# Gates and branch projections of a hybrid mixer: from weights on the partitions to tokens on the partitions

## The chip, the cores and the metric

The kernel runs on one core of one Trainium2 chip. The time is device time in microseconds of one execution, as the median of several runs of the same program. The engines are named as in the profile: PE is the matmul engine (PEld its weight loads), DVE the vector engine, ACT the scalar engine, POOL the general engine, and SP the engine whose queue issues the DMA transfers here. A matmul has a stationary operand of 128 x 128 (loaded by PEld) and a moving one with up to 512 columns that streams past it.

## The reference, cut to what matters

The model is a trunk of two layers on 256 tokens of width 1024. Each layer is a feed-forward network (FFN), a mixer block with three branches, and a second FFN. Of the mixer block this part is concerned:

```python
(z, xbc, dt_raw, rq, rk, rv, rg, aq, ak, av, gate) = jnp.split(h @ w_in[l], offsets, axis=-1)
y_ssd = ssd_mixer(...); y_ret = retention_mixer(...); y_att = swa_sink_attention(...)
ys = jnp.stack([y_ssd, y_ret, y_att], axis=2)
branch = jnp.einsum('blmc,mcd->blmd', ys, w_branch[l])
gates = jax.nn.sigmoid((gate + b_gate[l]).reshape(bsz, L, N_BRANCH, D_MODEL))
y = jnp.sum(gates * branch, axis=2) @ w_out[l]
x = x + rmsnorm(y, mix_post_g[l])
```

Here `h` is the normed input (256 x 1024), each of the three gates and of the three branch projections is a product of 256 x 1024 by 1024 x 1024, and the gated sum goes through one more such product, `w_out`.

## The kernel before

Everything is float32. A product is made of three matmuls on split operands: `split` (lines 65 to 68) makes a high part by a rounding copy on ACT and the rest by a subtraction on DVE, and `mm3` (85 to 89) adds low x high, high x high and high x low. So each k slot of 128 rows costs three matmuls, at lines 87, 88 and 89.

Weights are streamed once. `units` (70 to 83) loads 512 KB into a buffer `raw` (four of them) and splits it into a buffer `hl` (eight of them); one `hl` holds two k slots of 512 columns. The activations lie transposed in four tiles (`xT` for the normed input, `yT` for a branch's output, `ysT` for the gated sum), high and low part, with features on the partitions and all 256 tokens in the columns; `transposed` (138 to 149) makes such tiles on PE from a tile with tokens on the partitions, four transposes to a PSUM bank, and splits them on ACT and DVE.

There are two forms of a product. `gemm` (91 to 98) has 128 tokens as the stationary operand and 512 weight columns as the moving one; the result has tokens on the partitions. `gemmT` (100 to 105) has 128 weight columns as the stationary operand and all 256 tokens as the moving one; the result has features on the partitions.

In `mix`, the projections of the mixers come first. Their tasks run as generators that `pump` moves on a step after each product. Then a loop over the mixers (m = 2 attention, 1 retention, 0 SSD) makes the gate (two halves of 512 columns), finishes the mixer, transposes its output to `yT`, and makes the branch projection. Gates and branches are `gemmT` products: the gate's bias is then one number to a partition and goes into ACT's tanh (line 763), the gated sum `acc` has features on the partitions, and it needs only a split to be the operand `ysT` of the output projection. `close` (276 to 284) makes the output projection in four `gemm` products (half, token tile), and norms each token tile behind its second half; the next phase's opening norm and transposes (`prenorm`, 154 to 163) follow on it.

PSUM has five banks for products (`acc`) and three for the rest (`pst`). The rows of weights that are broadcast to all partitions, 512 KB each (`gain`, 115 to 118), share two buffers. The order of instructions on each engine is not the program's own: the tile framework sorts them by a simulated timeline when the program is built, and each engine then works in order. All loads go through SP's queue, in order.

Of the kernel before, what the change touches and what calls it, by code (L numbers as in the profile page):

```python
# [8 lines left out]
F32 = mybir.dt.float32  # L9
R = mybir.dt.float32r  # L10
AF = mybir.ActivationFunctionType
ALU = mybir.AluOpType
AX = mybir.AxisListType

P = 128
T = 256
NT = 2
# [22 lines left out]
class Trunk:  # L40
# [11 lines left out]
        self.pst = pool("pst", 3, space=bass.MemoryType.PSUM)  # L52
        self.gens = []

# [1 line left out]
    def t4(self, shape, dtype=F32, name="t4"):  # L56
        return self.big.tile([P] + shape, dtype, tag="t4", name=name, bufs=N4)

# [39 lines left out]
        return ps  # L98

    def gemmT(self, ps, xT, slots, c0):  # L100
        """the transposed product: 128 columns of the weight from c0 on, by all tokens"""
        for k, (wh, wl) in enumerate(slots):
            x = xT[k // 2]
            cs = slice(c0, c0 + P)
            self.mm3(ps, wh[:, cs], wl[:, cs], x[:, k % 2, 0], x[:, k % 2, 1], k == 0, k == len(slots) - 1)
# [97 lines left out]
    def pbank(self, dtype=F32):  # L203
        return self.pst.tile([P, 4, P], dtype, tag="pst", name="pb")

# [1 line left out]
    def setup(self):  # L207
        nc, A = self.nc, self.A
        self.ready = False
# [55 lines left out]
        return t  # L265

    def begin(self, gname, l):
        """norm and transposes that open a phase: returns the tiles and what does one token tile"""
        g = self.gain(gname, l)
        xT = self.new_T(4, "xT")  # L270
        return xT, lambda t: self.prenorm(xT, t, g)
# [2 lines left out]
        return sum((self.units(self.A[f"w_ffn{i}_out"][l], u, fine=u > 8) for u in range(11)), [])  # L274

    def close(self, order, gemm, gpost, scale, nxt):
        """output projection, residual update and the next phase's opening, token tile by token tile"""
        y = {}
        for n, t in order:
            y[t, n] = gemm(n, t)  # L280
            if n:
                self.postnorm(t, [y[t, 0], y[t, 1]], gpost, scale, 4 * EPS, nxt is None)
                if nxt:
                    nxt(t)
# [34 lines left out]
        self.nc.sync.dma_start(out=b, in_=src)  # L319
        return b  # L320

# [1 line left out]
    def att_kv(self, t, ps):  # L323
        nc, S = self.nc, self.S
        if t == 0:
# [95 lines left out]
        for t in range(NT):  # L421
            S[f"y2{t}"] = o[t].rearrange("p h d -> p (h d)")

# [1 line left out]
    def rotate(self, key, t, ps):  # L425
        nc, S = self.nc, self.S
        ps = ps.rearrange("p (h o d) -> p h o d", h=4, o=2)
# [81 lines left out]
            S[f"y1{t}"] = y  # L509

    def silu2(self, ps, dtype=F32, name="gz"):
        """2 * silu of a PSUM bank, in a new SBUF tile"""
        nc = self.nc
        g = self.t2([512], name=name)
        nc.scalar.activation(out=g, in_=ps, func=AF.Tanh, scale=0.5)
        nc.vector.scalar_tensor_tensor(out=g, in0=g, scalar=1.0, in1=ps, op0=ALU.add, op1=ALU.mult)
        return g

# [1 line left out]
    def ssd_dt(self):  # L520
        nc, S = self.nc, self.S
        x = S["dt"]
# [143 lines left out]
    def mixer_consts(self, l):  # L666
        nc, A = self.nc, self.A
        c = lambda n, w: self.sm.tile([P] + w, F32, tag="mc_" + n, bufs=1, name=n)
        bc = lambda ap: ap.partition_broadcast(P)
        self.sink, self.ea, self.dsk, self.dtb = (c(n, [16]) for n in ("sink", "ea", "dsk", "dtb"))  # L670
        for t, n in ((self.sink, "attn_sinks"), (self.ea, "a_log"), (self.dsk, "d_skip"), (self.dtb, "dt_bias")):
            nc.sync.dma_start(out=t, in_=bc(A[n][l]))
        nc.scalar.activation(out=self.ea, in_=self.ea, func=AF.Exp)
        self.bg = c("bg", [24])
        nc.sync.dma_start(out=self.bg, in_=A["b_gate"][l])
        nc.vector.tensor_scalar(out=self.bg, in0=self.bg, scalar1=0.5, scalar2=None, op0=ALU.mult)
        self.cw = c("cw", [12, 5])
        nc.sync.dma_start(out=self.cw, in_=A["w_conv"][l])
        nc.vector.tensor_scalar(out=self.cw, in0=self.cw, scalar1=0.5, scalar2=None, op0=ALU.mult)

    def mix(self, l, xT, nxt):
# [57 lines left out]
        for key in ("rg0", "rg1"):  # L739
            slots = W(ci)  # L740
            ci += 1
            for t in range(NT):
                main(key, t, slots)
        acc = [self.t4([4, T], name="ysum") for n in range(2)]
        ysT = []
        for m, gens in ((2, att), (1, ret), (0, ssd)):
            if m == 1:
                for key in ("z0", "z1"):
                    slots = W(ci)
                    ci += 1  # L750
                    for t in range(NT):
                        main(key, t, slots)
            gate = []
            for n in range(2):
                slots = W(ci)
                ci += 1
                for b in range(2):
                    ps = self.acc.tile([P, 2, T], F32, tag="acc", name="acc")
                    g = self.t2([2, T], name="gate")
                    for j in range(2):  # L760
                        c = 4 * n + 2 * b + j
                        self.gemmT(ps[:, j], xT, slots, (2 * b + j) * P)
                        nc.scalar.activation(out=g[:, j], in_=ps[:, j], func=AF.Tanh, scale=0.5,  # L763
                                             bias=self.bg[:, 8 * m + c:8 * m + c + 1])
                    gate.append(g)
                    self.pump()
                    if len(gate) == 2:
                        for gen in gens:
                            self.finish(gen)
                        yT = self.new_T(4, "yT")  # L770
                        for t in range(NT):
                            self.transposed(yT, S[f"y{m}{t}"], t)
            slots = sum((self.units(A["w_branch"][l], 4 * m + u) for u in range(4)), [])
            for i in range(4):
                ps = self.acc.tile([P, 2, T], F32, tag="acc", name="acc")
                for j in range(2):
                    self.gemmT(ps[:, j], yT, slots[8 * (i // 2):8 * (i // 2) + 8], (2 * (i % 2) + j) * P)
                g = gate[i]
                a = acc[i // 2][:, 2 * (i % 2):2 * (i % 2) + 2]
                if m == 2:  # L780
                    nc.vector.scalar_tensor_tensor(out=a, in0=g, scalar=1.0, in1=ps, op0=ALU.add, op1=ALU.mult)
                else:
                    nc.vector.scalar_tensor_tensor(out=g, in0=g, scalar=1.0, in1=ps, op0=ALU.add, op1=ALU.mult)
                    nc.vector.tensor_tensor(out=a, in0=a, in1=g, op=ALU.add)
                if m == 0:
                    y = self.new_T(1, "ysT")
                    self.split(y[0][:, :, 0], y[0][:, :, 1], a)
                    ysT += y
                self.pump()
        gpost = self.gain("mix_post_g", l)  # L790
        slots = sum((self.units(A["w_out"][l], u, fine=u > 1) for u in range(4)), [])
# [24 lines left out]
def host(inputs):  # L816
# [18 lines left out]
    out["w_out"] = pack(w, 512)  # L835
    cw = np.concatenate([f.pop("conv_w"), f.pop("conv_b")[:, None]], 1)
    out["w_conv"] = np.ascontiguousarray(cw.reshape(DEPTH, 5, 12, P).transpose(0, 3, 2, 1))
    out["b_gate"] = np.ascontiguousarray(f.pop("b_gate").reshape(DEPTH, 24, P).transpose(0, 2, 1))
    out.update(f)
    out.update(consts())  # L840
    out["c_ident"] = np.eye(P, dtype=np.float32)
# [1 line left out]


def consts():
    """Tables that depend on the shapes alone."""
    f = np.float32
    c = {}
    i = np.arange(P)
# [43 lines left out]
```

## Time and profile before

| | |
|---|---|
| median of 3 runs | 1545.32 us (1544.34 to 1547.5) |
| profiled execution, span from first to last instruction | 1548.9 us |
| PE busy | 1516.6 us (98%), 10122 matmuls |
| DVE busy | 973.1 us (63%) |
| ACT busy | 756.5 us (49%) |
| HBM read | 268.73 MB, 174 GB/s over the span |

The page has no time of the profiled execution other than its span. Busy times of PE overlap, since a matmul starts before the one ahead of it has left the array, so a full PE is not one at its peak. In the first layer the mixer block reaches from about 208 to 583 us, and its gates and branches, with the last projections between them, from about 389 to 561 us.

### The profile page before, as it was taken

Reading aid. Unit: us, or ns where it says so; the run is one execution under the profiler, and the core shown is the slowest. Engines: PE = TensorE matmul, PEld = TensorE weight load, DVE = VectorE, ACT = ScalarE, POOL = GpSimd, SP = SyncE. Lnnn points to the kernel's source line nnn. Section 1 sums busy time; section 2 is a strip of 40 time slices with the busy share of each in tenths; the row PEclk is TensorE's granted clock in tenths of the full one; section 3 lists DMA queues with packets and bytes.
Section 4 is the critical chain, followed back from the end, with each engine's and each line's share of the span. In section 5 each row is a group of like instructions: output and inputs, shape, how many; then the busy total and the mean of one; then the engine's idle time right before and its main releaser. Section 6 shows DMA issues by size and latency. Waiting matters only on the chain.

```text
span 1548.9 us, 25438 instructions
## 1 busy us (share of the span) xinstructions
PE 1516.6 (98%) x10122; PEld 1392.1 (90%) x10122; DVE 973.1 (63%) x1548; ACT 756.5 (49%) x1299; POOL 49.8 (3%) x72
## 2 busy tenths in 40 slices
PE   7999999999999999999999999999999999999998
PEld 5999878998989997999879998789989999789986
DVE  5554467788576666454564544777876776765553
ACT  6444456465445445454454543645545535554442
POOL 0000010001000001000010000100010000000000
PEclk9999999999999999999999999999999999999999
DMA  7555456535363546555555445654444545545452
GB/s 284 195 186 195 152 200 206 178 110 178 120 207 128 174 167 209 181 174 173 197 195 186 166 173 181 211 196 141 152 131 164 174 153 178 190 169 199 164 191 81
DMA packets 81111, 271.46 MB, mean 175 GB/s; under 512 B 10400, under 2 KB 15200, under 8 KB 80992
## 3 DMA queue, kind: packets, MB, share of 16 engines
q1 hardware_dynamic: 80992, 269.84, 51.3%
q8 instruction: 79, 1.29, 0.3%
q14 instruction: 40, 0.33, 0.1%
HBM read 268.73 MB, written 1.07 MB: 174 GB/s over the span
## 4 chain that ended last, share of the span: by engine, by line
PE 82%; issue 13%; DMA 1%; DVE 1%; ACT 1%; POOL 1%; SPq 0%; DVEq 0%; POOLq 0%; ACTq 0%
PE acc L87 23%; PE acc L89 23%; PE acc L88 23%; PE xbc L89 1%; PE xbc L87 1%; PE xbc L88 1%; PE po L416 1%; PE pT L146 1%; PE pS L383 1%; PE py L641 1%; DVE hl L68 1%; PE pb L408 1%; DMA raw<-w_ffn_in 1%; PE pb L634 0%; DMA gain<-ffn_pre_g 0%
## 5 line engine op out<-in xcount | busy, mean ns | idle before, releaser
L68 DVE TENSOR_TENSOR hl<-raw,hl 128x1024 fp32r<-128x1024 f32 (+2 forms) x544 | 583.4, 1104 | 291.1 <-ACT hl L67 285.4
L67 ACT CAST hl<-raw 128x1024 fp32r<-128x1024 f32 (+2 forms) x544 | 497.9, 952 | 326.3 <-PE acc L89 266.3
L87 PE MATMUL acc<-xT,hl 128*128 128x256 f32 x1536 | 435.8, 284 | 0.3 <-ACT gate L763 0.3
L89 PE MATMUL acc<-xT,hl 128*128 128x256 f32 x1536 | 435.8, 284 | 0.0
L88 PE MATMUL acc<-xT,hl 128*128 128x256 f32 x1536 | 435.4, 284 | 0.0
L87 PEld LDWEIGHTS acc<-xT,hl 128*128 128x128 f32 x1536 | 294.5, 192 | 2.0 <-issue 1.1
L88 PEld LDWEIGHTS acc<-xT,hl 128*128 128x128 f32 x1536 | 294.5, 192 | 0.6 <-issue 0.2
L89 PEld LDWEIGHTS acc<-xT,hl 128*128 128x128 f32 x1536 | 294.4, 192 | 0.2 <-issue 0.2
L87 PE MATMUL acc<-hl,xT 128*128 128x512 f32 (+1 forms) x480 | 192.1, 401 | 3.6 <-ACT xT L67 3.4
L88 PE MATMUL acc<-hl,xT 128*128 128x512 f32 (+1 forms) x480 | 188.7, 393 | 0.0
L89 PE MATMUL acc<-hl,xT 128*128 128x512 f32 (+1 forms) x480 | 186.2, 396 | 2.4 <-DVE xT L68 2.3
L87 PE MATMUL acc<-hl,hT 128*128 128x512 f32 x352 | 137.0, 389 | 0.0
L88 PE MATMUL acc<-hl,hT 128*128 128x512 f32 x352 | 137.0, 389 | 0.0
L89 PE MATMUL acc<-hl,hT 128*128 128x512 f32 x352 | 136.3, 389 | 0.0
L87 PEld LDWEIGHTS acc<-hl,xT 128*128 128x128 f32 x480 | 93.2, 194 | 22.2 <-ACT xT L67 5.5
L89 PEld LDWEIGHTS acc<-hl,xT 128*128 128x128 f32 x480 | 91.5, 192 | 23.6 <-DVE xT L68 6.0
L87 PE MATMUL acc<-yT,hl 128*128 128x256 f32 x384 | 109.5, 286 | 0.0
L88 PE MATMUL acc<-yT,hl 128*128 128x256 f32 x384 | 109.2, 285 | 0.0
L88 PEld LDWEIGHTS acc<-hl,xT 128*128 128x128 f32 x480 | 93.2, 194 | 17.4
L89 PE MATMUL acc<-yT,hl 128*128 128x256 f32 x384 | 108.2, 283 | 0.0
L112 DVE TENSOR_TENSOR h<-sl,acc 128x256 f32<-128x256 f32 x88 | 36.8, 418 | 85.5 <-ACT sl L110 85.2
L110 ACT ACTIVATE sl<-acc 128x256 f32<-128x256 f32 x88 | 33.5, 381 | 106.0 <-PE acc L89 105.5
(201 smaller groups left out, 1853.1 us busy)
## 6 DMA issues: line engine op xcount, KB each, us to landing
raw<-w_ffn_in SPq DMA_DIRECT2D x176, 512.0 KB, 4.7
raw<-w_main SPq DMA_DIRECT2D x152, 512.0 KB, 4.5
raw<-w_ffn_out SPq DMA_DIRECT2D x88, 512.0 KB, 4.8
raw<-w_branch SPq DMA_DIRECT2D x48, 512.0 KB, 4.6
raw<-w_out SPq DMA_DIRECT2D x16, 512.0 KB, 5.0
bias<-rows SPq DMA_DIRECT2D x8, 512.0 KB, 5.8
raw<-w_kvdt SPq DMA_DIRECT2D x8, 272.0 KB, 2.9
gain<-ffn_pre_g SPq DMA_DIRECT2D x4, 512.0 KB, 4.3
```

The lines of the kernel that those rows point to most:

```text
L67: nc.scalar.copy(out=hi, in_=src)
L68: nc.vector.tensor_tensor(out=lo, in0=src, in1=hi.bitcast(F32), op=ALU.subtract)
L87: mm(ps, xh, wl, start=start, stop=False)
L88: mm(ps, xh, wh, start=False, stop=False)
L89: mm(ps, xl, wh, start=False, stop=stop)
L110: nc.scalar.activation(out=sl, in_=a, func=AF.Silu)
L112: nc.vector.tensor_tensor(out=h, in0=sl, in1=b, op=ALU.mult)
L146: nc.tensor.transpose(ps[:, j], src[:, (q + j) * P:(q + j + 1) * P], self.ident)
L383: nc.tensor.matmul(pS[:, i, :w], qT[t][:, hb + j + i], kT[:, g, hl, ks], start=hl == 0, stop=hl == 1)
L408: nc.tensor.transpose(pp[:, j], s[:, j, b * P:b * P + P], self.ident)
L416: nc.tensor.matmul(po[:, j], pT[b][:, j], vt[:, vo + b, 64 * g:64 * g + 64], start=b == 0, stop=b == t)
L641: nc.tensor.matmul(py[:, j], L[:, j], xdt[t][:, 8 * g + j], start=True, stop=True)
```

## The change

Gates and branch projections become `gemm` products, with tokens on the partitions. A bank then holds one token tile by 512 columns. The bias of the gate now differs along the columns: it is loaded as a `gain` tile of 128 x 1024, one for each mixer, added on DVE, and then tanh follows on ACT. The small tile `bg` with its load and scaling is gone. The gated sum `acc` has tokens on the partitions, and for the last mixer each finished half of a token tile is transposed on PE and split into `ysT`. The last mixer's branch products go token tile by token tile, those of the others half by half. The split of the weights, their loads and the output projection are as before. The other lines of the diff take out comments only.

```diff
-        self.bg = c("bg", [24])
-        nc.sync.dma_start(out=self.bg, in_=A["b_gate"][l])
-        nc.vector.tensor_scalar(out=self.bg, in0=self.bg, scalar1=0.5, scalar2=None, op0=ALU.mult)
...
-        acc = [self.t4([4, T], name="ysum") for n in range(2)]
-        ysT = []
+        acc = [self.t4([D], name="ysum") for t in range(NT)]
+        ysT = self.new_T(4, "ysT")
...
-            gate = []
+            bg = self.gain("b_gate", l, m * D)
+            gate = {}
             for n in range(2):
                 slots = W(ci)
                 ci += 1
-                for b in range(2):
-                    ps = self.acc.tile([P, 2, T], F32, tag="acc", name="acc")
-                    g = self.t2([2, T], name="gate")
-                    for j in range(2):
-                        c = 4 * n + 2 * b + j
-                        self.gemmT(ps[:, j], xT, slots, (2 * b + j) * P)
-                        nc.scalar.activation(out=g[:, j], in_=ps[:, j], func=AF.Tanh, scale=0.5,
-                                             bias=self.bg[:, 8 * m + c:8 * m + c + 1])
-                    gate.append(g)
+                for t in range(NT):
+                    ps = self.gemm(xT, t, slots)
+                    g = gate[n, t] = self.t2([512], name="gate")
+                    nc.vector.tensor_tensor(out=g, in0=ps, in1=bg[:, 512 * n:512 * n + 512], op=ALU.add)
+                    nc.scalar.activation(out=g, in_=g, func=AF.Tanh, scale=0.5)
                     self.pump()
...
-            slots = sum((self.units(A["w_branch"][l], 4 * m + u) for u in range(4)), [])
-            for i in range(4):
-                ps = self.acc.tile([P, 2, T], F32, tag="acc", name="acc")
-                for j in range(2):
-                    self.gemmT(ps[:, j], yT, slots[8 * (i // 2):8 * (i // 2) + 8], (2 * (i % 2) + j) * P)
-                g = gate[i]
-                a = acc[i // 2][:, 2 * (i % 2):2 * (i % 2) + 2]
+            u = [self.units(A["w_branch"][l], 4 * m + i) for i in range(4)]
+            order = [(n, t) for n in range(2) for t in range(NT)] if m else [(n, t) for t in range(NT) for n in range(2)]
+            for n, t in order:
+                ps = self.gemm(yT, t, u[2 * n] + u[2 * n + 1])
+                g = gate[n, t]
+                a = acc[t][:, 512 * n:512 * n + 512]
...
                 if m == 0:
-                    y = self.new_T(1, "ysT")
-                    self.split(y[0][:, :, 0], y[0][:, :, 1], a)
-                    ysT += y
+                    self.transposed(ysT[2 * n:2 * n + 2], a, t)
```

How the built order changes is shown at three places of the first layer. The numbers in names tell buffers apart.

First, PE's queue at the end of the last branch product (`acc<-yT`) and the start of the output projection (`acc<-ysT`). Before:

```order
L88 MATMUL acc_5763<-yT_5400,hl_5598 128x256
L89 MATMUL acc_5763<-yT_5400,hl_5598 128x256
L87 MATMUL acc_5873<-hl_5821,ysT_5652 128x512
L88 MATMUL acc_5873<-hl_5821,ysT_5652 128x512
L89 MATMUL acc_5873<-hl_5821,ysT_5652 128x512
```

And now, 11 matmuls into the output projection, where the first half of token tile 1 of the gated sum is transposed:

```order
L89 MATMUL acc_5328<-hl_5281,ysT_3873 128x512
L87 MATMUL acc_5328<-hl_5281,ysT_3873 128x512
L88 MATMUL acc_5328<-hl_5281,ysT_3873 128x512
L146 MATMUL pT_5227<-identr_86,ysum_3871 128x128 x4
L89 MATMUL acc_5328<-hl_5281,ysT_3873 128x512
```

Transposes of the sum are new in PE's queue; two of the four groups stand in the last branch product, and two in the output projection.

Second, PE's queue inside the output projection, where `acc_5873`, `acc_5898` and `acc_5968` are its first, second and third product. Before:

```order
L87 MATMUL acc_5898<-hl_5848,ysT_5706 128x512
L88 MATMUL acc_5898<-hl_5848,ysT_5706 128x512
L89 MATMUL acc_5898<-hl_5848,ysT_5706 128x512
L87 MATMUL acc_5968<-hl_5821,ysT_5652 128x512
L87 MATMUL acc_5898<-hl_5848,ysT_5706 128x512
```

And now, with `acc_5353` as the second product and `acc_5423` as the third:

```order
L89 MATMUL acc_5353<-hl_5317,ysT_3875 128x512
L87 MATMUL acc_5353<-hl_5317,ysT_3875 128x512
L88 MATMUL acc_5353<-hl_5317,ysT_3875 128x512
L89 MATMUL acc_5353<-hl_5317,ysT_3875 128x512
L87 MATMUL acc_5423<-hl_5276,ysT_3872 128x512
```

Before, five matmuls of the third product stood ahead of the end of the second, and 43 matmuls of the projection behind it; now the third starts behind it, and 48 stand there.

Third, DVE's queue where the first gates (those of attention) are made; `cb` is a product of the SSD, `st` and `mv` belong to the retention's norm. Before:

```order
L593 TENSOR_TENSOR xdt<-px,dt 128x512
L595 TENSOR_TENSOR xsd<-px,dsk 128x512
L610 TENSOR_TENSOR cb<-pb,triur 128x512
L494 BN_STATS st<-po 128x6 x2
L495 BN_AGGR mv<-st 128x2 x2
```

And now:

```order
L595 TENSOR_TENSOR xsd<-px,dsk 128x512
L68 TENSOR_TENSOR hl<-raw,hl 128x1024 x2
L610 TENSOR_TENSOR cb<-pb,triur 128x512
L758 TENSOR_TENSOR gate<-acc,gain 128x512 x2
L68 TENSOR_TENSOR hl<-raw,hl 128x1024
L494 BN_STATS st<-po 128x6 x2
```

Two bias additions stand behind `cb`, ahead of a split of branch weights and of the retention's norm, and three such splits that stood further back come earlier.

## Rows read from the trace of the kernel before

**Rows 1.** The page's first two parts: busy us (share) xinstructions; granted clock in tenths.

```profile
PE 1516.6 (98%) x10122; PEld 1392.1 (90%) x10122; DVE 973.1 (63%) x1548; ACT 756.5 (49%) x1299; POOL 49.8 (3%) x72
...
PEclk9999999999999999999999999999999999999999
```

**Rows 2.** Windows of the first layer's stage: from:to, length, busy us of each engine.

```profile
380.00:572.00 192.00, 191.72 (x1433) 182.72 (x1432) 126.15 (x168) 88.44 (x140) 5.04 (x6) 1.00 0.50 166
440.00:460.00 20.00, 20.00 (x112) 17.38 (x110) 16.72 (x18) 10.86 (x15) 0.00 (x0) 1.00 0.61 205
```

**Rows 3.** Timeline of PE, transposed branch product: start us, us, engine, line, operation.

```profile
559.79 0.28 PE L87 MATMUL acc<-yT,hl 128*128 128x256 f32 x1
...
561.11 0.28 PE L89 MATMUL acc<-yT,hl 128*128 128x256 f32 x1
561.23 0.40 PE L87 MATMUL acc<-hl,ysT 128*128 128x512 f32 x1
```

**Rows 4.** Timeline of PE, output projection of the first FFN.

```profile
199.83 0.39 PE L89 MATMUL acc<-hl,hT 128*128 128x512 f32 x1
...
205.95 0.39 PE L89 MATMUL acc<-hl,hT 128*128 128x512 f32 x1
```

**Rows 5.** Instructions by line and shape: xcount | busy us, mean ns of one.

```profile
L87 PE MATMUL acc<-yT,hl 128*128 128x256 f32 x384 | 109.5, 286 | 0.0
```

**Rows 6.** Transposes in the chain that ended last: start us, us.

```profile
470.70 0.87 PE pT L146 x8
...
475.89 0.44 PE pT L146 x4
```

**Rows 7.** Line 146: durations in ns min/median/max, first and last start.

```profile
L146 PE MATMUL pT<-identr,xsd x32: 270/272/273, 519.2 to 1299.1; 128*128 128x128 f32 x32
```

**Rows 8.** Waits from 380 to 572 us: us in total, times, longest.

```profile
PEld acc L87 <- ACT gate L763: 0.5, 1, 0.5
...
PE acc L87 <- ACT gate L763: 0.3, 1, 0.3
```

**Rows 9.** Instructions by line and shape, on DVE and ACT.

```profile
L171 DVE TENSOR_TENSOR yg<-acc,gain 128x512 f32<-128x512 f32 x24 | 16.2, 688 | 30.8 <-PE acc L89 30.7
L763 ACT ACTIVATE gate<-acc,bg 128x256 f32<-128x256 f32 x48 | 22.4, 472 | 46.3 <-PE acc L89 46.3
L515 ACT ACTIVATE gz<-acc 128x512 f32<-128x512 f32 x16 | 9.5, 595 | 17.1 <-PE acc L89 17.1
L68 DVE TENSOR_TENSOR ysT<-ysum,ysT 128x512 fp32r<-128x512 f32 x8 | 5.5, 690 | 2.7 <-ACT ysT L67 2.7
L68 DVE TENSOR_TENSOR xT<-pT,xT 128x256 fp32r<-128x256 f32 x48 | 19.4, 421 | 8.4 <-ACT xT L67 8.1
```

**Rows 10.** Timeline of DVE where the gates of attention begin.

```profile
381.47 0.69 DVE L710 TENSOR_TENSOR gz<-gz,gain 128x512 f32<-128x512 f32 x1
...
387.31 0.69 DVE L610 TENSOR_TENSOR cb<-pb,triur 128x512 f32<-128x512 f32 x1 [2.66 <-PE pb L608]
...
396.00 4.63 DVE L68 TENSOR_TENSOR hl<-raw,hl 128x1024 fp32r<-128x1024 f32 x4 [4.50 <-ACT hl L67]
```

**Rows 11.** Timeline of SP's queue at the same place.

```profile
382.19 0.33 SPq L117 DMA_DIRECT2D gain<-mix_post_g  x1
```

**Rows 12.** The page's part 6: DMA issues, KB each, us to landing.

```profile
gain<-ffn_pre_g SPq DMA_DIRECT2D x4, 512.0 KB, 4.3
```

**Rows 13.** Timeline of PE at the openings of both second FFNs.

```profile
584.62 1.32 PE L146 MATMUL pT<-identr,xn 128*128 128x128 f32 x8 [1.44 <-DVE xn L161]
...
1348.62 0.39 PE L89 MATMUL acc<-hl,ysT 128*128 128x512 f32 x1
1350.45 1.32 PE L146 MATMUL pT<-identr,xn 128*128 128x128 f32 x8 [1.44 <-DVE xn L161]
```

**Rows 14.** Windows of three phase openings: granted clock third from the end.

```profile
586.00:593.00 7.00, 6.37 (x14) 4.63 (x15) 5.85 (x11) 4.35 (x13) 1.22 (x2) 0.51 0.91 292
780.00:788.00 8.00, 6.45 (x18) 4.82 (x17) 6.60 (x13) 4.35 (x12) 2.24 (x4) 0.57 0.80 261
975.00:979.00 4.00, 3.84 (x12) 2.89 (x13) 3.57 (x7) 1.77 (x6) 1.93 (x2) 0.57 0.97 339
```

More of the change, by code (lines that the diff above doesn't have):

```diff
@@ L756, in mix @@
                 ci += 1
-                for b in range(2):
-                    ps = self.acc.tile([P, 2, T], F32, tag="acc", name="acc")
-                    g = self.t2([2, T], name="gate")
-                    for j in range(2):
-                        c = 4 * n + 2 * b + j
-                        self.gemmT(ps[:, j], xT, slots, (2 * b + j) * P)
-                        nc.scalar.activation(out=g[:, j], in_=ps[:, j], func=AF.Tanh, scale=0.5,
-                                             bias=self.bg[:, 8 * m + c:8 * m + c + 1])
-                    gate.append(g)
-                    self.pump()
[L767 to L772, printed above, removed]
-            slots = sum((self.units(A["w_branch"][l], 4 * m + u) for u in range(4)), [])
-            for i in range(4):
-                ps = self.acc.tile([P, 2, T], F32, tag="acc", name="acc")
-                for j in range(2):
-                    self.gemmT(ps[:, j], yT, slots[8 * (i // 2):8 * (i // 2) + 8], (2 * (i % 2) + j) * P)
-                g = gate[i]
-                a = acc[i // 2][:, 2 * (i % 2):2 * (i % 2) + 2]
+                for t in range(NT):
[3 more added lines that the diff above has]
+                    nc.scalar.activation(out=g, in_=g, func=AF.Tanh, scale=0.5)
+                    self.pump()
+                if n == 0:
+                    for gen in gens:
+                        self.finish(gen)
+                    yT = self.new_T(4, "yT")
+                    for t in range(NT):
+                        self.transposed(yT, S[f"y{m}{t}"], t)
+            u = [self.units(A["w_branch"][l], 4 * m + i) for i in range(4)]
[4 more added lines that the diff above has]
+                a = acc[t][:, 512 * n:512 * n + 512]
                 if m == 2:
@@ L837, in host @@
     out["w_conv"] = np.ascontiguousarray(cw.reshape(DEPTH, 5, 12, P).transpose(0, 3, 2, 1))
-    out["b_gate"] = np.ascontiguousarray(f.pop("b_gate").reshape(DEPTH, 24, P).transpose(0, 2, 1))
     out.update(f)
```

## The prediction

> **What bounds the kernel now.** I read the page's first two parts, then windows of the changed stage, then PE's timeline in it. PE is busy 98% of the span, and the granted clock is in its top tenth in all 40 slices [rows 1]; in the stage that is changed, from 380 to 572 us of the first layer, PE is busy for 191.7 of 192.0 us while DVE is busy for 126 and ACT for 88 [rows 2]. So the stage costs what PE's queue of matmuls costs, and busy time is the wrong measure of that, because matmuls overlap: a 256-column one is shown as 0.28 us long, but the next starts 0.12 us later. What counts is the step from start to start. Between 559.79 and 561.11 us lie 11 steps of the transposed product, so 0.120 us each [rows 3]; between 199.83 and 205.95 us lie 27 steps of the 512-column product that a projection with tokens on the partitions uses, so 0.2267 us each [rows 4]. Two 256-column steps are 0.240 us, one 512-column step 0.2267 us. Per column that is (226.7 - 120) / 256 = 0.417 ns, one column per cycle at 2.4 GHz, and each matmul pays about 13 ns beside its columns.
>
> **The gates and branch projections.** Each of the 12 products per layer (three mixers, gate and branch, two halves of 512 columns) was 4 column blocks x 8 weight slots x 3 = 96 matmuls of 256 columns; now it is 2 token tiles x 8 x 3 = 48 of 512. The branch half alone is 3 x 384 = 1152 matmuls in the whole program [rows 5], and the gates are as many, so 2304 x 0.120 = 276.5 us becomes 1152 x 0.2267 = 261.2 us: **-15.3 us**. Every one of these stands in PE's queue, and PE was hardly ever held in the stage, so I count all of it.
>
> That the 13 ns are paid per matmul rests on the trace alone [rows 3, 4]. The Trainium skill, in "TensorE: Matmul & The Clock Gate", section "Back-to-back issue gap", gives N / 2.4 + 2.5 ns for a warm matmul: by it the saving would be only 1152 x 2.5 ns = 2.9 us (an estimate from that page), and the whole sum -1.4 us. The trace differs from the page by about 11 ns per matmul, and the measurement decides.
>
> **The sum's transposes.** The gated sum now has its tokens on the partitions and must be turned for the output projection: 2 token tiles x 2 halves make 4 groups of 4 transposes a layer, 32 transposes in all. A group of 4 takes 0.44 us on the chain, and 8 take 0.87 [rows 6]: 8 groups x 0.44 = **+3.5 us**. From below the bound is 0 if PE would else stand idle there, which the stage's 0.3 us of idle time excludes. From above, a group could also make the queue drain once; the longest hold of PE by a neighbour in the first layer's mixer, 0.5 us [rows 8], would make it 8 x 0.94 = 7.5 us. I take 3.5, since the groups stand between other matmuls in the new order.
>
> The Trainium skill, same page, "Part 4: PE-mode transpose", names about 275 ns for one in a kernel's context; 32 x 0.275 would be +8.8 us (an estimate from the page) and the sum -8.5 us. The row's duration, 272 ns [rows 7], agrees, but it is an overlapped one: eight of them take 0.87 us on the chain.
>
> Where the transposes stand matters, because PE works in order. For the last mixer the branch product goes by token tile. By the new order the four groups stand 26, 24, 35 and 38 matmuls behind the last one of the product that they turn: DVE has at least 24 x 0.2267 = 5.4 us for the two operations of a gated sum, some 0.7 us each by the nearest form [rows 9], with a weight split or two between. So I count no wait there.
>
> **DVE and ACT.** Added on DVE: 24 additions of the gate bias, a PSUM bank with a 128x1024 gain tile, the same form as the post-norm's 0.688 us: +16.5 us. The split of the turned sum becomes 16 of 0.42 instead of 8 of 0.69: +1.2 us. On ACT 48 tanh of 0.472 us, two to a tile, become 24 of 512 columns at 0.595 us: 22.7 us go to 14.3 [rows 9]. DVE in the stage goes from 126 of 192 us to about 135 of 185, 73%; its fullest slice, 440 to 460 us, is at 16.7 of 20 [rows 2]. So DVE stays off the path on average; I cost this at **0**, hidden behind the matmuls. Without that cover it is up to 0.7 us for each addition, 16.5 us.
>
> Each addition now stands ahead of weight splits in DVE's queue and waits for its product, and the first also for the bias. That bias takes the place of the retention gain, whose last use ends at 382.1 us; in the kernel before another load went out at 382.19 us, as soon as that buffer was free. A gain of 512 KB lands in 4.3 us, so at about 386.5 us. The first two additions stand right behind an operation for which DVE waited until 387.31 us anyway, and the next weights were split from 396.00 us on [rows 10 to 12]. So I see about 8 us of room. The five other biases wait for the last addition of the one before, and in SP's queue each stands among weight loads that wait for later events; cost 0.
>
> **The output projection's opening.** Before, the second product (half 1, tile 0) was interleaved with the third, and ended 43 matmuls before the end; now the two stand apart and 48 follow it. Tile 0's norm, and from it the first transposes of the next phase, hang on that end: PE stood idle for 1.44 us at 584.62 us and again for 1.44 us at 1350.45 us [rows 13]. Five more matmuls cover 1.13 us of it if the chain of norms keeps its length; bounds 0 and 1.13 us a layer. I take 1.0: **-2.0 us**.
>
> **Sum.** -15.3 + 3.5 - 2.0 = -13.8 us against the profiled execution's 1548.9 us span, so 1535.1. The page has no time of that execution but its span, and the timed runs have a median of 1545.32, 3.6 us less. A likely reason: three phase openings ran partly at 1.2 GHz, the half clock. A mean of 0.51 over 7 us is 6.9 us at half clock, 0.57 over 8 us is 6.9 us again, and 0.57 over 4 us is 3.4 us [rows 14]; half of such a time is lost, so 3.4 us at a long one, and a run with one less would be at 1545.5. Measured against the median I predict 1545.3 - 13.8 = **1531.5 us**.
>
> **Rivals.**
> - *Half is given back* (1538.4 us, chance 0.20). The transposes drain the queue (+4.0 us, to the bound of 7.5), the phase openings gain nothing (+2.0 us), and some of the gate additions come late for PE (two of 0.5 us): -13.8 + 7.0 = -6.8. For it: the queues were put in order for guessed durations, and PE works in order. Against: PE was held in this stage for 0.3 us only.
> - *The extra time per matmul does not go away* (1546.8 us, chance 0.08). If the 13 ns come from what the stage does beside PE and not from each matmul, the columns are the same as before and only +3.5 - 2.0 = +1.5 us is left. For it: just as many columns are streamed. Against: the 0.2267 us is measured in an output projection with the same splits on DVE and ACT. The Trainium skill's rule on the issue gap, cited above, lies near this case: 1543.9 us by its figure.
> - *The bias loads hold the weights up* (slower, 1549.5 us, chance 0.08). There are two gain buffers, one is held by the SSD norm, so the next bias can't be requested until the last addition of the one before; SP works in order, and a load that waits there holds all weight loads behind it. If each of the 6 loads puts the next weights off by as much as 3.0 us (below the 4.3 us that a gain takes to land), that is +18 - 13.8 = +4.2 us. It decides from 2.3 us per load on. Against: eight split weight tiles stand ready, 8 x 12 x 0.2267 = 21.8 us of PE's work when full.
>
> **Numbers.** Forecast 0.64, the others 0.20, 0.08, 0.08. A difference under 0.2%, 3.1 us, can't be told from none here. Faster by more: 0.64 + 0.20 = 0.84; within: 0.08, with a share of the borders 0.09; slower: 0.07. The forecast's own range is one half-clock opening, 3.4 us, to either side, with 0.6 us more below: 1527.5 to 1535. The range for 8 in 10 is 1527 to 1540, so that it takes in the half-lost case.
>
> **What would show it.** In the new trace: 0.227 us from start to start in gates and branches; 32 transposes of the sum in groups of 0.44 us; PE's idle time at the opening of both second FFNs at about 0.4 us instead of 1.44; DVE near 73% in the stage, with the additions waiting for PE and not PE for them. I am wrong if PE's holds in the stage grow by more than a few us, above all weight loads waiting behind a bias, or if the step is not 0.227.

## The result, and the profile after

The changed kernel takes 1532.5 us (median of 4 runs, 1531.9 to 1532.8) where the kernel before took 1544.9 beside it (4 runs): a ratio of 0.9901, with a 95% interval of 0.9885 to 0.9918. Forecast were 1531.5 us and 13.8 us less; it was 12.4 us less.

First the page of the changed kernel: its part 1 (busy us, share, instructions) and, from its part 6, the loads of the new bias (KB each, us to landing).

```profile
PE 1498.0 (98%) x9002; PEld 1331.0 (87%) x9002; DVE 989.5 (65%) x1578; ACT 757.9 (50%) x1283; POOL 43.0 (3%) x72
...
gain<-b_gate SPq DMA_DIRECT2D x6, 512.0 KB, 6.1
```

Beside [rows 1] PE issues 1120 matmuls fewer: 1152 saved in the products, 32 transposes added. PE's share is 98% as before; that share could not have told the gain. Next, the gate product of the last mixer, in PE's timeline (start us, us, engine, line, operation):

```profile
514.80 0.39 PE L89 MATMUL acc<-hl,xT 128*128 128x512 f32 x1
...
518.88 0.39 PE L89 MATMUL acc<-hl,xT 128*128 128x512 f32 x1
```

18 steps in 4.08 us, 0.2267 us each: the step that [rows 4] had promised. And the first group of the sum's transposes, in the same view, with the one row that sums up all 32 of them (durations min/median/max in ns, first and last start):

```profile
564.73 0.39 PE L88 MATMUL acc<-hl,ysT 128*128 128x512 f32 x1
564.97 0.60 PE L146 MATMUL pT<-identr,ysum 128*128 128x128 f32 x4
565.32 0.48 PE L89 MATMUL acc<-hl,ysT 128*128 128x512 f32 x1
565.63 0.40 PE L87 MATMUL acc<-hl,ysT 128*128 128x512 f32 x1
```

```profile
L146 PE MATMUL pT<-identr,ysum x32: 269/272/273, 544.5 to 1319.7; 128*128 128x128 f32 x32
```

A transpose lasts 272 ns by its row, but from the matmul before the group to the second one behind it are 0.90 us, where without the group there would be 2 steps, 0.45 us: the group of four costs 0.45 us.

Then the two engines that the change loads. Instructions by line and shape (count, busy us, mean ns, and what ended the idle time before them), and windows of the first layer's stage (from:to, length, busy us of PE, PEld, DVE, ACT and POOL, granted clock), which answer to [rows 9] and [rows 2]:

```profile
L758 DVE TENSOR_TENSOR gate<-acc,gain 128x512 f32<-128x512 f32 x24 | 16.4, 686 | 10.9 <-PE acc L89 10.9
L759 ACT ACTIVATE gate<-gate 128x512 f32<-128x512 f32 x24 | 15.1, 632 | 16.4 <-DVE gate L758 16.4
```

```profile
378.00:556.00 178.00, 178.00 (x846) 147.78 (x845) 130.83 (x175) 87.55 (x128) 5.99 (x8) 1.00 0.54 178
440.00:460.00 20.00, 20.00 (x104) 17.04 (x103) 14.79 (x15) 9.74 (x14) 0.00 (x0) 1.00 0.56 178
208.00:216.00 8.00, 7.79 (x29) 6.17 (x28) 6.15 (x10) 2.88 (x10) 3.03 (x4) 0.57 0.61 230
578.00:590.00 12.00, 9.70 (x47) 7.89 (x46) 10.04 (x18) 7.80 (x17) 1.72 (x4) 1.00 0.86 299
1333.00:1345.00 12.00, 9.81 (x47) 7.79 (x46) 9.32 (x17) 7.65 (x17) 1.72 (x4) 1.00 0.77 277
```

PE is busy in all of the 178.00 us and the view of waits shows none of PE's in them; DVE is busy for 130.83, 73.5%, and its additions wait for PE for 10.9 us, never the other way. The last three windows are needed below: the one phase opening behind the first 14 us of this execution that ran at the half clock (0.57 at 208 us), and the openings of both second FFNs, which here ran at full clock.

**Where the time went.** The two traces, cut in PE's timeline at the start of an output projection's first and last matmul, and at the first gate (us; layer 1, layer 2; the first stretch begins with PE's first transpose at 10 us):

```
stretch                                        before            after
gates and branches, to the output projection   184.91, 184.35    178.37, 178.35
output projection of the mixers                 21.56,  21.56     22.49,  22.49
second FFN, to its output projection           134.38, 133.41    130.97, 131.11
first FFN, to its output projection            136.21, 135.03    135.20, 133.04
mixers, to the first gate                      170.38, 171.21    172.42, 170.24
each FFN's output projection                    59.64,  59.64     59.64,  59.64
```

The stage and its projection give -12.5 + 1.9 = -10.7 us. The rest of the 17.9 us between the two spans (1548.9 and 1531.0) lies in phase openings, and part of that is clock. Behind its first products the execution before had 6.8 us at the half clock at 586 us, 6.8 at 781 and 3.4 at 975 [rows 14], and 3.4 more at 23 us:

```profile
23.00:26.40 3.40, 3.40 (x8) 2.25 (x9) 2.49 (x8) 3.39 (x9) 0.00 (x0) 0.50 0.95 368
```

The one after had 6.8 us at 208 us. So the stage, its projection and the second FFN of layer 2 are at full clock in both traces, and they give -10.7 - 2.3 = -13.0 us. The five stretches with a half-clock spell in one of the two give -5.3 us together, of which the second FFN of layer 1 has -3.4, and the two ends of the span give +0.4. How much of the -5.3 is the change's the two traces alone don't tell; more on it below.

For the same reason the runs of one kernel spread: by a straight line through each kernel's runs (span against mean granted clock) they are 0.6 to 1.2 us shorter with a mean granted clock 0.001 higher, and 0.84 in the 16 runs of the kernel before. (The six runs of "raw5", all within 0.002 of clock, give 2.3.) These lines, read at 0.996, set the kernels side by side better than medians of few runs. Runs of the kernel before are those of the first set below, without one of 3495 us; the 11 of the second set give 1545.5:

```
kernel      runs   span at clock 0.996   against the changed kernel
before        16         1545.4                 +14.5
changed        4         1530.9
again          5         1530.9                   0.0
half          12         1546.3                 +15.4
noturn         4         1527.5                  -3.4
nobias         4         1531.6                  +0.7
nmajor         4         1531.3                  +0.4
ffn            5         1526.5                  -4.4
raw5           6         1531.6                  +0.7
ffn_raw5       4         1527.7                  -3.2
```

### The profile page after: what moved, and what is told of

Read it like the earlier page. It is cut to its first block, busy times and chain, and to the rows that moved or that the text cites. A ratio compares the mean times of both kernels' runs of the same rounds, so it can differ in the third digit from the quotient of the medians.

```text
span 1531.0 us, 23233 instructions
## 1 busy us (share of the span) xinstructions
PE 1498.0 (98%) x9002; PEld 1331.0 (87%) x9002; DVE 989.5 (65%) x1578; ACT 757.9 (50%) x1283; POOL 43.0 (3%) x72
## 4 chain that ended last, share of the span: by engine, by line
PE 82%; issue 13%; DMA 2%; DVE 2%; ACT 1%; POOL 0%; SPq 0%; POOLq 0%; DVEq 0%; ACTq 0%
PE acc L89 23%; PE acc L87 23%; PE acc L88 23%; PE xbc L89 2%; PE xbc L87 2%; PE xbc L88 2%; PE po L416 1%; PE pT L146 1%; DMA raw<-w_ffn_in 1%; DVE hl L68 1%; PE pS L383 1%; PE py L641 1%; PE pb L408 1%; DMA raw<-w_main 1%; PE pb L634 0%
## 5 line engine op out<-in xcount | busy, mean ns | idle before, releaser
L67 ACT CAST hl<-raw 128x1024 fp32r<-128x1024 f32 (+2 forms) x544 | 504.3, 954 | 342.4 <-PE acc L89 256.3
L87 PE MATMUL acc<-xT,hl 128*128 128x256 f32 x1152 | 326.8, 284 | 0.0
L88 PE MATMUL acc<-xT,hl 128*128 128x256 f32 x1152 | 326.7, 284 | 0.0
L89 PE MATMUL acc<-xT,hl 128*128 128x256 f32 x1152 | 326.6, 284 | 0.0
L87 PE MATMUL acc<-hl,xT 128*128 128x512 f32 (+1 forms) x672 | 265.9, 396 | 7.7 <-ACT xT L67 6.6
L88 PE MATMUL acc<-hl,xT 128*128 128x512 f32 (+1 forms) x672 | 261.9, 390 | 0.0
L89 PE MATMUL acc<-hl,xT 128*128 128x512 f32 (+1 forms) x672 | 259.9, 393 | 1.6 <-DVE xT L68 1.5
L87 PEld LDWEIGHTS acc<-xT,hl 128*128 128x128 f32 x1152 | 221.3, 192 | 0.8 <-issue 0.6
L88 PEld LDWEIGHTS acc<-xT,hl 128*128 128x128 f32 x1152 | 221.4, 192 | 0.2
L89 PEld LDWEIGHTS acc<-xT,hl 128*128 128x128 f32 x1152 | 221.4, 192 | 0.0
L87 PEld LDWEIGHTS acc<-hl,xT 128*128 128x128 f32 x672 | 127.7, 190 | 34.3 <-ACT xT L67 8.9
L89 PEld LDWEIGHTS acc<-hl,xT 128*128 128x128 f32 x672 | 126.5, 189 | 28.7 <-DVE xT L68 3.7
L88 PEld LDWEIGHTS acc<-hl,xT 128*128 128x128 f32 x672 | 127.7, 190 | 24.1 <-issue 0.2
L89 PEld LDWEIGHTS acc<-hl,hT 128*128 128x128 f32 x352 | 66.1, 188 | 13.7
L88 PEld LDWEIGHTS acc<-hl,hT 128*128 128x128 f32 x352 | 66.1, 188 | 13.6
L87 PEld LDWEIGHTS acc<-hl,hT 128*128 128x128 f32 x352 | 66.1, 188 | 13.6
```

The lines of the kernel that those rows point to most:

```text
L67: nc.scalar.copy(out=hi, in_=src)
L87: mm(ps, xh, wl, start=start, stop=False)
L88: mm(ps, xh, wh, start=False, stop=False)
L89: mm(ps, xl, wh, start=False, stop=stop)
```

## The experiments

Each diff is against the changed kernel. Two sets ran, each beside its own runs of the kernel before (medians of 1548.39 and 1547.76 us). My theory was the prediction's: a cost paid for each matmul beside its columns, so that half as many matmuls of twice the width save it. The rival was that the gain is in the form (tokens on the partitions, what DVE and ACT do with it, the new order), and not in the width.

**half: the new layout with the old width.**

```diff
+    def gemm2(self, xT, t, slots):
...
+        for j in range(2):
+            cs = slice(256 * j, 256 * j + 256)
+            for k, (wh, wl) in enumerate(slots):
+                x = xT[k // 2]
+                self.mm3(ps[:, cs], x[:, k % 2, 0, ts], x[:, k % 2, 1, ts], wh[:, cs], wl[:, cs], k == 0, k == n - 1)
...
-                    ps = self.gemm(xT, t, slots)
+                    ps = self.gemm2(xT, t, slots)
...
-                ps = self.gemm(yT, t, u[2 * n] + u[2 * n + 1])
+                ps = self.gemm2(yT, t, u[2 * n] + u[2 * n + 1])
```

> The changed kernel, but each gate and branch product is made in two halves of 256 columns: 96 matmuls of 256 instead of 48 of 512, with tokens still on the partitions, and DVE, ACT, transposes and loads as in the changed kernel. Theory A (each matmul pays 13 ns beside its columns): 1152 x 0.2267 = 261.2 us becomes 2304 x 0.120 = 276.5 us, so +15.3 us on 1532.5: 1547.8, with 0.120 us from start to start whichever operand is the moving one. Rival B (the gain came from the order of the work, the openings of phases or the clock, and not from the number of matmuls): about 1532.5 to 1535. In between would say that the step of 0.120 us hangs on what is stationary.

Measured: 1547.87 us (12 runs), 0.9994 of the kernel before (0.9982 to 1.0007). The whole gain is gone, with layout, bias additions, transposes and order all kept. PE's timeline of this kernel, in the last branch product:

```profile
559.82 0.28 PE L89 MATMUL acc<-hl,yT 128*128 128x256 f32 x1
...
560.54 0.28 PE L89 MATMUL acc<-hl,yT 128*128 128x256 f32 x1
560.66 0.40 PE L87 MATMUL acc<-hl,ysT 128*128 128x512 f32 x1
```

Six steps in 0.72 us: 0.120 us as in [rows 3], now with the tokens and no longer the weights as the operand that is loaded. So the cost beside the columns hangs on the number of matmuls and not on which operand stands still. The stage takes 185.23 and 185.22 us instead of 178.37 and 178.35, 13.7 us more for 1152 more matmuls: 11.9 ns each. Over the whole span at equal clock it is 15.4 us, 13.4 ns each; the trace of the stage is the surer of the two. So the rival has fallen as the account of the gain. One part of the form does pay: in this kernel the second FFNs up to their output projections take 131.47 and 131.06 us at full clock, where the kernel before has 133.41 in layer 2. That gain and the price of the transposes (below) about cancel here.

**noturn: the sum is split as it stands, without transposes.**

```diff
-                    self.transposed(ysT[2 * n:2 * n + 2], a, t)
+                    ts = slice(t * P, t * P + P)
+                    for j in range(2):
+                        d = ysT[2 * n + j]
+                        self.split(d[:, :, 0, ts], d[:, :, 1, ts],
+                                   a[:, 256 * j:256 * j + 256].rearrange("p (k n) -> p k n", k=2))
```

> The changed kernel without the 32 transposes of the gated sum: the sum is split as it lies into the operand of the output projection, so the output is not the reference's; the splits on ACT and DVE keep their number and size. Theory A (a transpose costs PE 0.109 us in its queue and nothing else): -3.5 us, 1529.0. Rival (the transposes also hold PE up, or lengthen the way to the output projection): up to -7.5 us, 1525.0. Rival (the opening of the next phase is bound by its weights, so that a shorter output projection is waited for there): less than -3.5, about 1531.5, with longer idle time before the first matmuls of both second FFNs.

Measured: 1531.15 us (4 runs), ratio 0.9892 (0.9877 to 0.9906). Its median is only 1.4 us below the first one of the changed kernel, but its runs had a mean clock of 0.9933; at equal clock it is 3.4 us faster. The trace gives it without that: the stage is 0.96 us shorter in each layer (177.41 and 177.39), the projection 0.96 too (21.53), so 3.84 us for 8 groups, 0.48 us a group. PE's timeline of this kernel in the output projection shows plain steps where a group stood:

```profile
564.67 0.39 PE L89 MATMUL acc<-hl,ysT 128*128 128x512 f32 x1
564.90 0.39 PE L87 MATMUL acc<-hl,ysT 128*128 128x512 f32 x1
565.12 0.39 PE L88 MATMUL acc<-hl,ysT 128*128 128x512 f32 x1
```

**nobias: no bias load and no addition.**

```diff
-            bg = self.gain("b_gate", l, m * D)
...
-                    nc.vector.tensor_tensor(out=g, in0=ps, in1=bg[:, 512 * n:512 * n + 512], op=ALU.add)
-                    nc.scalar.activation(out=g, in_=g, func=AF.Tanh, scale=0.5)
+                    nc.scalar.activation(out=g, in_=ps, func=AF.Tanh, scale=0.5)
```

> The changed kernel without the gate's bias: ACT's tanh reads the bank, the 24 additions on DVE and the six loads of 512 KB are gone (the output lacks that bias). Theory A (the additions are hidden behind the matmuls): 1532.5, within 1 us either way. Rival (they hold weight splits up in DVE's queue, or their loads hold the weights up): faster by a part of 16.5 us, at least 2 us, with less idle time of PE between the first gate and the output projection (178.4 us in both layers of the changed kernel).

Measured: 1533.36 us (4 runs), ratio 0.9904 (0.989 to 0.9919). The stage takes 178.32 and 178.34 us, where it took 178.37 and 178.35. At equal clock the kernel is no faster either. The 24 additions on DVE, 16.4 us of its time, and the six loads cost nothing that can be measured: cover and bias rival are both settled.

**nmajor: the last mixer by halves, as the others.**

```diff
-            order = [(n, t) for n in range(2) for t in range(NT)] if m else [(n, t) for t in range(NT) for n in range(2)]
+            order = [(n, t) for n in range(2) for t in range(NT)]
```

> The changed kernel, but the last mixer's branch products go half by half as those of the others, not token tile by token tile. Theory A (the order only gives DVE and ACT time to finish token tile 0 before the output projection; 24 matmuls, 5.4 us, are enough in either order): within 1 us of 1532.5. Rival (half 1 of token tile 0 is finished one product later, and its transposes, splits and the projection's weights come too late): +1 to +4 us, with idle time of PE at the start of the output projection.

Measured: 1533.59 us (4 runs), ratio 0.9901 (0.9886 to 0.9916). The groups of transposes move between the two stretches (178.82 and 22.04 us), but their sum is the same to 0.01 us: 200.86 (layer 1; layer 2 200.84 in both). The order inside that product is worth nothing; PE has no wait there in either order.

**ffn: the same change for the FFNs' remaining chunks.** In the changed kernel these still run 256 columns wide; here they go by token tile, 512 wide, with a transpose of each h.

```diff
-            if c < 2:
+            if True:
```

> The changed kernel with the same step taken in the four FFNs: chunks 2 to 10 of the first projection are made with tokens on the partitions too (48 matmuls of 512 columns instead of 96 of 256), and the hidden tile is transposed on PE, as chunks 0 and 1 were before. Theory A: 9 x 4 x 96 = 3456 matmuls of 256 become 1728 of 512, 1728 x (0.240 - 0.2267) = -23.0 us; 9 x 4 x 4 = 144 transposes at 0.109 to 0.12 us add 15.7 to 17.3 us: -5.7 to -7.3 us, about 1526 beside 1532.5. Rival (a transpose stands on the way from a product to its hidden tile, and PE waits for swiglu in it): no gain, or slower by up to 72 holds of 0.4 us less 6.5 us, +22 us.

Measured: 1528.22 us (5 runs, 1527.33 to 1531.89), ratio 0.9883 (0.9865 to 0.99): faster than both kernels, by 5.1 us against the median of the run "again" beside it, and by 4.4 at equal clock. That is less than the theory's sum. Instructions of this kernel by line and shape, and then its waits on PE (us in total, times, longest):

```profile
L89 PE MATMUL acc<-hl,xT 128*128 128x512 f32 x1216 | 482.6, 399 | 0.0
...
L146 PE MATMUL pT<-identr,h 128*128 128x128 f32 x176 | 33.5, 271 | 0.9 <-DVE h L112 0.9
```

```profile
PE pT L146 <- DVE xn L161: 14.5, 5, 9.3
PE acc L87 <- ACT xT L67: 6.6, 6, 2.0
PE pT L146 <- DVE h L112: 0.9, 1, 0.9
```

The 3 x 1152 matmuls of 256 columns have become 3 x 576 of 512, and 144 of the 176 transposes of h are new. At the 11.9 ns of the run "half" the products save 1728 x 11.9 = 20.6 us; 4.4 are left, so 16.2 us are given back, 0.22 us for each of the 72 new groups of two transposes. PE's timeline has one such group in the middle of a product:

```profile
640.54 0.39 PE L88 MATMUL acc<-hl,xT 128*128 128x512 f32 x1
640.78 0.38 PE L146 MATMUL pT<-identr,h 128*128 128x128 f32 x2
640.91 0.48 PE L89 MATMUL acc<-hl,xT 128*128 128x512 f32 x1
641.23 0.39 PE L87 MATMUL acc<-hl,xT 128*128 128x512 f32 x1
```

From the matmul before the group to the second one behind it are 0.69 us, where two steps are 0.45: 0.24 us. One group stands inside each FFN's output projection, which is 0.25 us longer for it. The only wait for h, 0.9 us, was there before the change. So the change pays where few transposes go with many matmuls saved (32 with 1152 in gates and branches), and little here (144 with 1728).

**raw5 and ffn_raw5: a fifth buffer for raw weights**, alone and with the change above. They test what the phase openings wait for (see below).

```diff
-        self.rawp = pool("raw", 4)
+        self.rawp = pool("raw", 5)
```

> The changed kernel with five buffers for raw weights instead of four. It is about the opening of phases, where PE now waits 2.3 us for a cast that stands in ACT's queue behind casts of weights that wait for their loads. Theory C (the opening is bound by how early its weights can be asked for): one load more under way takes about 1 to 2 us off each of five openings, -5 to -10 us. Rival (the loads come as fast as HBM gives them in that stretch, with a DMA share of 0.86): within 1 us of 1532.5, with the same 2.3 us.

> Both of the last two edits together. If both theories hold, the sum of their gains: about 1518 to 1521. If only theory A holds: about 1526. If the transposes cost what the matmuls save: 1532.

Measured: 1535.13 us (6 runs), ratio 0.9912 (0.9897 to 0.9928), and 1529.61 us (4 runs), ratio 0.9884 (0.9868 to 0.99). No gain in either over the whole program. PE's waits at the opening of the first layer's second FFN in raw5:

```profile
PE acc L87 <- ACT xT L67: 1.9, 1, 1.9
PE acc L89 <- DVE xT L68: 1.2, 1, 1.2
```

The wait for the cast of xT is still there, 1.9 us instead of 2.3 (3.4 us of this opening ran at the half clock), and one of 1.2 us has come behind it. So the fifth buffer does not shorten this opening. But it does not leave everything as it was: with no half-clock spell behind the first 16 us, the first FFN of layer 1 up to its output projection takes 132.97 us in raw5, where the changed kernel, "half" and "nobias" take 134.65 to 135.20. The second FFN of layer 1 takes 133.41 us with a half-clock spell of 3.4 us, where the second FFNs of "noturn", "nobias", "nmajor" and "again" with such a spell take 132.16 to 132.60. So one opening gains and another loses; why isn't shown.

**again: the changed kernel once more, beside the last three.**

> The changed kernel itself, on the chip of these three and with more runs, to read its time against the granted clock of each run. Theory D (the runs of one kernel differ by the share of half clock at the openings, 0.8 to 0.9 us for each 0.001 of mean clock, as the kernel before shows it in 16 runs from 0.988 to 0.998): the spans of the changed kernel lie 14 to 15 us below those of the kernel before at the same mean clock. Rival (the clock is no part of it): no slope of the span over the clock, and the 12.4 us between the medians is the whole effect.

Measured: 1533.36 us (5 runs), ratio 0.9904 (0.9888 to 0.9919), and the stage again 178.37 and 178.35 us. At a mean clock of 0.996 its runs lie 14.6 us below those of the kernel before beside it, with a slope of 1.2 us for each 0.001 (0.85 there): theory D holds, with a somewhat steeper slope. Within the stage the trace repeats to 0.01 us; the openings don't: the second FFN of layer 2 took 132.60 us, where the first profile has 131.11. Here its first product began at the half clock (a granted clock of 0.50, third from the end):

```profile
1336.90:1340.30 3.40, 3.34 (x8) 2.70 (x9) 2.59 (x5) 2.26 (x7) 0.66 (x2) 0.50 0.97 329
```

## Why the prediction came out right, step by step

**Gates and branches (-15.3 us forecast).** Right in mechanism, some 10% too large. The step of 0.2267 us and its count are as read, and "half" shows the cause. But not every step is as short as the ones in the middle of a product. In the stage 672 steps of 512 columns a layer (576 of the new products and 96 of the SSD gate's) have a mean of 231.3 ns, 155.4 us in all: some 80 of them take 231 to 236 ns, and those next to small matmuls are longer still. Before, 1152 steps of 256 had a mean of 121.9 ns and the 96 of 512 one of 227.4, 162.2 us in all. So the term was -6.8 us in the first layer and, counted in the same way, -7.0 in the second, -13.8 for both, where I had multiplied the shortest step by all. (Another 0.7 us was gained at the small matmuls between the products: stage and projection without the transposes' 3.84 us give -14.5.) The Trainium skill's figure of 2.5 ns ("TensorE: Matmul & The Clock Gate", "Back-to-back issue gap") would have made the saving 2.9 us, an estimate; the runs show 11.9 to 13.4 ns per matmul, as the trace of before did. That section of the Trainium skill gives the figure for isolated matmuls, and for a stream in which each matmul has a weight load about 131 ns at 512 columns; the steps here, 226.7 ns, are far above that too, and the measurement decides.

**Transposes (+3.5 us).** Right: 3.84 by "noturn", 0.48 us a group instead of 0.44, between the bounds of 0 and 7.5, and with no wait of PE behind them.

**DVE and ACT (0).** Right, and tested by "nobias". The forecast share of 73% is 73.5. Each bias took 6.1 us to land and not the 4.3 of [rows 12]; that was inside the room that I had counted as 8 us.

**The second FFN's opening (-2.0 us, by an idle time of 0.4 instead of 1.44 us).** This is the step whose mechanism failed, and its size was too small. PE's timeline of the changed kernel, where [rows 13] had the wait of 1.44 us:

```profile
578.37 0.39 PE L89 MATMUL acc<-hl,ysT 128*128 128x512 f32 x1
578.60 1.03 PE L146 MATMUL pT<-identr,xn 128*128 128x128 f32 x8
581.94 0.50 PE L87 MATMUL acc<-hl,xT 128*128 128x512 f32 x1 [2.30 <-ACT xT L67]
```

The wait for the norm is not 0.4 us: it is gone, and the transposes follow the last matmul in one step. But a wait of 2.30 us for the cast of the turned tile has taken its place, and ACT's timeline says why:

```profile
576.00 1.15 ACT L67 CAST hl<-raw 128x512 fp32r<-128x512 f32 x2 [0.24 <-DMA raw<-w_ffn_in]
578.33 1.14 ACT L67 CAST hl<-raw 128x512 fp32r<-128x512 f32 x2 [1.18 <-DMA raw<-w_ffn_in]
580.48 1.14 ACT L67 CAST hl<-raw 128x512 fp32r<-128x512 f32 x2 [1.01 <-DMA raw<-w_ffn_in]
581.52 0.36 ACT L67 CAST xT<-pT 128x256 fp32r<-128x256 f32 x1
```

The turned tile was ready at about 579.6 us (578.60 + 1.03), but its cast stands in ACT's queue behind weight casts which wait for their loads, and starts at 581.52. I had looked at the norm's chain alone and not at what is queued on ACT ahead of the next operation in that chain. Over the whole program the waits of PE, first before and then after, show the exchange:

```profile
PE pT L146 <- DVE xn L161: 18.0, 7, 10.1
PE acc L87 <- ACT xT L67: 3.4, 5, 1.6
PE acc L89 <- DVE xT L68: 2.3, 3, 1.3
```

```profile
PE pT L146 <- DVE xn L161: 15.3, 5, 10.3
PE acc L87 <- ACT xT L67: 6.6, 5, 2.3
PE acc L89 <- DVE xT L68: 1.5, 2, 0.8
```

Two waits of 1.4 us for xn have gone, and those for xT's cast have grown by 3.2 us. That something is gained all the same is due to later steps of the opening. The second FFN of layer 2 shows it, since it ran at full clock in both traces. Behind the wait for xn [rows 13] the kernel before waited twice more, for the low part of xT from DVE; the changed kernel waits once:

```profile
1354.45 0.50 PE L89 MATMUL acc<-hl,xT 128*128 128x512 f32 x1 [1.27 <-DVE xT L68]
...
1358.24 0.50 PE L89 MATMUL acc<-hl,xT 128*128 128x512 f32 x1 [0.78 <-DVE xT L68]
```

```profile
1336.19 0.50 PE L87 MATMUL acc<-hl,xT 128*128 128x512 f32 x1 [2.19 <-ACT xT L67]
```

The first product starts as long behind the projection's last matmul as it did (3.45 us, and 3.36 before), but the transposes now stand 1.7 us further ahead of it, and the low parts are ready when PE asks for them. The stretch fell from 133.41 to 131.11 us, -2.3 for this layer alone. The 132.60 of the run "again" is no second measure of it, since 3.4 us of it ran at the half clock; at full clock the changed kernel's second FFN took 130.80 us in layer 1 of that run and 130.97 in the first profile. For layer 1 no trace of the kernel before shows the opening at full clock. If it would take the 133.41 us of layer 2, then its 6.8 us at the half clock cost only 134.38 - 133.41 = 1.0 us, since the slower steps took the place of waits (0.7 us for xT there, 2.2 in layer 2), and the change brought -2.4 us there too. That is an estimate; with it the term is -4.7 for both layers, more than double of my -2.0.

**The base.** I had taken the profiled execution to lie 3.6 us above the median. In every run that lists both, the time is 1.8 us more than the span, so by that it lay 5.4 us above. And I had counted half of all half-clock time as lost. By the line through the 16 runs 0.84 us go with 0.001 of mean clock, which is 3.1 us at the half clock in a span of 1549: about a quarter. The 5.4 us would then take a mean clock of 0.998 instead of the profile's 0.992, inside the 0.988 to 0.998 of those runs, but the clocks of the runs behind that median aren't on record. The forecast stood on the median, and so it doesn't hang on this.

**The sum.** -10.7 us for stage and projection and -2.3 to -4.7 for the openings make -13.0 to -15.4 us, beside -12.4 between the medians and -14.5 at equal clock. The last has an uncertainty of about 2 us, as "half" shows: +15.4 by that line, 13.7 by the trace of its stage. That the forecast of -13.8 lies among these is in part luck: the products' steps brought 1.5 us less than forecast, and the openings 0.3 to 2.7 us more, in a way that I had not foreseen.

**The rivals.** That the extra time would stay was excluded by the step in the trace and by "half". That the bias loads would hold the weights up was excluded by PE's lack of waits and by "nobias". Of the half-given-back case (whose time adds up to 1538.5 us, not 1538.4) little came: the transposes cost 0.3 us more than forecast and not 4.0, no addition held PE, and the openings gained.

**What stays open.** What sets the end of the openings' waits. The casts on ACT wait for loads of w_ffn_in, and a fifth buffer did not shorten the second FFNs. A kernel in which xT's cast stands ahead of chunk 1's weight casts wasn't tried. And each matmul here comes with a weight load of its own (9002 of each), in "half" too, so no run tells whether the 12 ns belong to the matmul or to that load.

## What to carry to other kernels

Where PE is never held, count steps from start to start and not busy time: a fixed cost per matmul shows as the difference between two widths, and halving the number of matmuls was worth nearly that here (13.8 us of 15.3). What the wider form added on other engines was free where PE's waits stayed empty; the transposes it needs on PE were not, so count the groups against the matmuls saved. When a wait at a phase opening is to be taken away, look at the queues of all engines in the chain behind it: the next operation may be ready and still stand behind work that waits for a load.

## What the runs showed that I had not expected

Besides its columns a matmul pays 12 to 13 ns here, whichever operand stands still (0.120 us at 256 columns in [rows 3] and in "half", 0.2267 at 512). The two profiled executions differ by some 3 us more than the kernels do at equal clock (17.9 and 14.5 us), so a difference between two profiles can overstate or hide a part of a change of 1%; the stretches between openings repeat to 0.01 us and are the better measure, and of two openings only those with the same half-clock spells can be compared. The time at the half clock cost about a quarter of itself and not half; at the one opening looked at, it stood in the place of waits of PE. And a queued cast that waited for a load held PE longer (2.3 us) than the chain of norms that it follows had done (1.4 us).
